# Transposing two steps behind the scores, fetching stored activations by single parts, and stores from a second queue, in a two-layer encoder trunk on one core

## The chip, the core and the metric

The program runs on one of the eight cores of a Trainium2 chip. A core has TensorE (PE in the profile; its weight loads are PEld), VectorE (DVE), ScalarE (ACT), GpSimd (POOL) and SyncE (SP). The metric is the device time of one execution in microseconds (us); lower is better. For one core there are the times of three runs of the kernel before, and one more run under the hardware profiler, from which every row below comes.

## The reference

An encoder trunk of two layers works on two requests of 1024 tokens by 1024 channels that share all weights (`x_prompt` and `x_sample`). All data is 32-bit.

```python
def _trunk(x, c, ...):                       # for each of the two requests
    for i in range(2):
        shift, scale, gate = split(silu(c) @ w_mod[i] + b_mod[i], 3)
        h = _rmsnorm(x, norm_pre[i]) * (1.0 + scale) + shift
        y = _even_mixer(h, ...) if i == 0 else _odd_mixer(h, ...)
        x = x + gate * _rmsnorm(y, norm_post[i])
    return x
def _even_mixer(h, w_in, w_out, ...):        # layer 0
    q, k, v, ga, ub, gb = split(h @ w_in)    # 4 retention heads of 128, 32 S5 groups of 16
    o_a = _head_norm(_retention(_rotary(q), _rotary(k), v)) * silu(ga)
    o_b = _s5(ub, ...) * silu(gb)
    return concatenate([o_a, o_b], -1) @ w_out
def _odd_mixer(h, w_in, w_out, rel_bias):    # layer 1: 16 heads of 64 on a 16 x 64 grid
    q, k, v, g = split(h @ w_in, 4)
    s = q k^T * scale + bias                 # 8 rows x 16 columns of neighbours
    return (softmax(s) @ v * silu(g)) @ w_out
```

## The kernel before

**Products.** Every product with a large weight is made of three: a weight block comes in as `wr`, ScalarE makes `wh` from it (line 198), VectorE or GpSimd the rest `wl = wr - wh` (line 209), and TensorE adds `h_hi wh + h_lo wh + h_hi wl` (`mm`, line 131, 24 instructions for 512 tokens). The normalised input of a layer lies in `h_hi` and `h_lo`, one pair of 1024 tokens for one request at a time.

**Order.** Python generators stand for the secondary work. `spawn(gen, delay)` puts one in a list, and `unit()`, called after each dense product, takes one step of each; a step that yields n rests for n units. So the dense products of a stage are woven with one step each of the mixers. Most of the program is issued in the order in which it is written (`pin`); the rest is placed by a scheduler that moves instructions whose order isn't pinned.

**Stages.** First both requests are normalised, request 1 in `first` and request 0 in `make_h`; `h_rows` (lines 455 to 460) turns a block of x by TensorE, ScalarE applies scale and shift into a tile `tm`, VectorE and GpSimd make `h_hi` and `h_lo` of it, and for request 1 the tile is also stored to `hD[0]`. Beside them go the modulation products `psa<-wn` and `psc<-wn` of `mod`, whose last part calls `save_gate`, which stores a column of `mods` to `gD`; the projections `ub`, whose results `u` are stored to `uD`; and the parameters of the S5 mixer (`s5_params`), which go through DRAM (`ppD`) and are read back by the generator `s5`, which is woven into layer 0. The queue of SyncE issues all loads and all stores, one after the other, and each waits there until its data or its place is ready (the queue is SPq in the profile, line 191).

When request 0 is through its projections in layer 0, `load_h` brings request 1 back from `hD[0]`: four parts of 256 channels for each half of 512 tokens; each goes to a tile `hraw`, ScalarE copies it to `h_hi` (line 198) and VectorE or GpSimd subtracts to `h_lo` (line 438). Its three places in layer 0 (`hraw`, A12 A13 A14) are those of `kT`, `qT` and `ga` of the retention. Layer 1 does the same from `hD[1]` with `down=True`, there between requests 1 and 0 with a turned grid.

**Layer 1.** `na_dense` makes q, k and the gate of a pair of heads, `na_values` the values of two pairs, and the generator `na_mix` does the attention of one block of 128 queries of a pair of heads in each step: `na_scores` makes the scores in two banks `psa`; VectorE adds the bias and finds the largest (line 1203), ScalarE takes the exponential and its sum (line 1205), VectorE the reciprocal and the product (lines 1206 and 1207); one step later `na_turn` lets TensorE transpose the result into banks `psb` (line 136), and ScalarE and VectorE copy them to tiles `pt` (lines 198 and 1223); then products `psc` with the values are made for two blocks at once. The last steps run beside the output projection of layer 1 (`out_proj`), in which each unit has 12 products of 128 x 512; its own work on VectorE and GpSimd stands in lines 1116 and 1117.

Of the kernel before, what the change touches and what calls it, by code (L numbers as in the profile page):

```python
# [19 lines left out]
P = 128  # L20
# [8 lines left out]
ROWS, WIDE, EDGE = 16, 368, 256  # L29
# [9 lines left out]
def _parts(text):  # L39
# [31 lines left out]
    vn0=_fulls("A15"), kn=_fulls("A16"), vn1=_fulls("A17"), stf=_fulls("A18"), stb=_fulls("A6"),  # L71
    hraw=_fulls("A12 A13 A14"),
    gy=_fulls("E0 E1"), gz=_fulls("A11 A12 A13 A14"), ghl=_fulls("E2 E3"), gw=_fulls("A0 A1 A3 A4"))
# [44 lines left out]
class Trunk:  # L118
# [70 lines left out]

    def load(self, dst, src, pin=False):  # L190
        i = self.nc.sync.dma_start(dst, src)  # L191
        if pin:
            self.tc.keep_in_program_order(i)

    store = load

    def copy_a(self, dst, src, scale=1.0):
# [96 lines left out]
    def mod(self, l, t):  # L294
        pa = [self.pst("a"), self.pst("c")]
        for n in range(4):
            for h in range(2):
                w = self.t([P, 4, 256], "wn")
                c0 = t * 1024 + 256 * n
                self.load(w, self.I["w_mod"][l, 512 * h:512 * h + 512, c0:c0 + 256].rearrange("(k p) c -> p k c", p=P), pin=True)  # L300
                for k in range(4):
                    self.mm(pa[n // 2][32 * k:32 * k + 32, 256 * (n % 2):256 * (n % 2) + 256], self.cs[:, 4 * h + k], w[:, k],
                            start=(h == 0), stop=(h == 1))
                yield
        r = self.t([P, 1024], "modr")
        for n in range(2):
            self.copy_a(r[:, n * 512:(n + 1) * 512], pa[n])
        p2 = self.pst("b")[:, 0:16].rearrange("p (f s) -> p f s", f=8)
        for f in range(8):
            self.mm(p2[:, f], r[:, f * P:(f + 1) * P], self.sel, start=True, stop=True)  # L310
        self.mod_col(p2, l, t, slice(0, 8))
        if t == 2:
            self.save_gate(l)

# [103 lines left out]

    def load_h(self, saved, after, down=False):

        for half in range(2):
            sl = slice(half * 512, half * 512 + 512)
            for c in range(4):
                raw = self.t([P, 2, 512], "hraw")
                ks = slice(2 * c, 2 * c + 2)
                hi, lo = self.h_hi[:, ks, sl], self.h_lo[:, ks, sl]
                src = saved[256 * c:256 * c + 256]
                if down:
                    for k in range(2):
                        self.load(raw[:, k].rearrange("p (r c) -> p r c", r=ROWS),  # L430
                                  src[k * P:(k + 1) * P].rearrange("p (r c) -> p r c", r=ROWS)[:, :, 32 * half:32 * half + 32])
                    raw = raw.rearrange("p k (r c) -> p k c r", r=ROWS)
                    hi, lo = (z.rearrange("p k (c r) -> p k c r", r=ROWS) for z in (hi, lo))
                else:
                    self.load(raw, src[:, sl].rearrange("(k p) t -> p k t", p=P))
                self.copy_a(hi, raw)
                e = self.nc.gpsimd if c % 2 else self.nc.vector
                e.tensor_tensor(lo, raw, hi.bitcast(F32), SUB)
            yield after

# [6 lines left out]
    def h_rows(self, l, s, g, xs, fs, tags, save=None):  # L447
        nc, Vv = self.nc, self.nc.vector
        sl = slice(g * 512, (g + 1) * 512)
        for f in fs:  # L450
            pt = self.pst(tags[f % len(tags)])
            for i, x in enumerate(xs):
                self.tr(pt[:, i * P:(i + 1) * P], x[:, f * P:(f + 1) * P], self.ident)
            tm = self.t([P, 512], "tm")
            nc.scalar.activation(tm, pt, AF.Identity, bias=self.mods[:, l, 0, f, s:s + 1],
                                 scale=self.mods[:, l, 1, f, s:s + 1])
            hh = self.h_hi[:, f, sl]
            Vv.tensor_copy(hh, tm)  # L458
            e = nc.gpsimd if f % 2 else Vv
            e.tensor_tensor(self.h_lo[:, f, sl], tm, hh.bitcast(F32), SUB)  # L460
            if save is not None:
                self.store(save[f * P:(f + 1) * P, sl], tm, pin=True)

# [55 lines left out]
    def s5_params(self):  # L519
# [138 lines left out]
        V.tensor_copy(pkb[:, :, 32:64], o_im.rearrange("p (a g) i -> p a (g i)", g=2))  # L658
        ppv = self.ppD.rearrange("a p x -> p a x")
        for o, z in ((0, pkb), (128, pkw), (182, pkt)):  # L660
            self.store(ppv[:, :, o:o + z.shape[2]], z)

# [131 lines left out]

    def s5(self):

        st = self.s5_begin(0)
        self.s5_tables(st)
# [21 lines left out]
    def ub(self, s):  # L820
        def item(m):
# [7 lines left out]
            def done():  # L829
                self.store(self.uD[s][m * P:(m + 1) * P].rearrange("i t c -> i (t c)"),  # L830
                           u[0].rearrange("p t c -> p (t c)"))

# [230 lines left out]
    def out_proj(self, l, s, blks, xsrc, xdst, save=None):  # L1063
        nc = self.nc
        gp = None
        for i in range(8):
# [27 lines left out]
            if not l:  # L1094
                self.unit()
            gp = gp or self.gate_row(l, s)
            x = self.t([P, 1024], "ox")
# [63 lines left out]
    def na_start(self):  # L1161
# [5 lines left out]
        for a in range(2):  # L1167
            oth = slice(64 - 64 * a, 128 - 64 * a)
            for _ in range(2):
                self.nc.gpsimd.memset(self.t([P, 1024], f"kl{a}")[oth], 0.0)  # L1170
                self.nc.gpsimd.memset(self.t([P, 384], f"s{a}")[:, WIDE:], 0.0)

# [54 lines left out]
    def na_mix(self):  # L1227
# [3 lines left out]
        n = 8 * 16  # L1231
        for i in range(-2, n + 2):
            k, j = divmod(i + 2, 8)
            if k < 16:
# [8 lines left out]
                elif j == 3 and k < 15:  # L1243
                    raw = self.na_raw((k + 1) % 8)
            if i >= 3 and i % 2:
                for b in (i - 3, i - 2):
                    k, j = divmod(b, 8)
# [9 lines left out]
                if j % 4 == 3:  # L1257
# [3 lines left out]
                    self.store(self.oD[1, s][p * P:(p + 1) * P, sl], o)  # L1261
            if 0 <= i - 1 < n:
                pts[i - 1] = self.na_turn(sbs.pop(i - 1), (i - 1) % 8)
            if 0 <= i < n:
# [49 lines left out]
    def layer0(self, xin):  # L1314
# [22 lines left out]
        self.project(ub[1][2:], "2")  # L1337
        self.s5_params()
        ph, self.ph = self.ph, Phase(MAP_L0, **banks)
        self.xs = [self.t([P, 4, P], f"xs{i}") for i in range(2)]  # L1340
        self.bm = self.t([P, 2, 2, 48], "bm")
        for x in self.xs + [self.bm]:
            nc.gpsimd.memset(x, 0.0)
        self.spawn(self.s5(), 4)
        self.ph, ph = ph, self.ph
# [7 lines left out]
        for s in range(2):  # L1353
# [10 lines left out]
            if s == 0:  # L1364
                self.spawn(self.load_h(self.hD[0], 3), 4)
                self.project(gb[0], "13")
# [23 lines left out]
    def layer1(self):  # L1390
# [19 lines left out]
        for s in range(2):  # L1410
            for p in range(8):
# [3 lines left out]
                if s == 0 and p == 7:  # L1415
                    self.spawn(self.load_h(self.hD[1], 3, True), 2)
                if s == 1 and p == 7:
# [89 lines left out]
```

## Time and profile before

| | us |
|---|---|
| runs | 2287.92, 2291.08, 2293.56 |
| median | 2291.08 |
| profiled execution | 2285.23 |
| its span, first to last instruction | 2283.5 |
| TensorE busy in it | 2183.2 (96%) |
| VectorE busy | 1371.3 (60%) |
| ScalarE busy | 850.4 (37%) |
| GpSimd busy | 786.0 (34%) |

The profiled execution is one of its own beside the three runs. Busy time counts the instructions of an engine, so what is missing from the span of TensorE is time in which it had none to do; whether it worked at its full clock is told by PEclk, the granted share of 2.4 GHz.

### The profile page before, as it was taken

How to read it: one execution, taken by the hardware profiler on the slowest of the kernel's cores; microseconds unless marked ns; L12 is line 12 of the kernel's file. 1: busy time of each engine (PE TensorE's matmuls, PEld its weight loads, DVE VectorE, ACT ScalarE, POOL GpSimd, SP SyncE). 2: the span in 40 equal slices, each digit the busy share in tenths (PEclk: the TensorE clock that was granted, in tenths of full speed). 3: DMA queues.
4: the chain of work that ended last, by engine and by line, in shares of the span. 5: the costliest groups of instructions: out<-in, count | busy, mean ns of one | idle time of the engine just before them, and what ended most of it. 6: DMA issues, size and time to landing. Idle time of an engine off the chain costs nothing.

```text
span 2283.5 us, 35173 instructions
## 1 busy us (share of the span) xinstructions
PE 2183.2 (96%) x13248; PEld 1838.0 (80%) x13248; DVE 1371.3 (60%) x3013; ACT 850.4 (37%) x1842; POOL 786.0 (34%) x670
## 2 busy tenths in 40 slices
PE   6989998998999999999999999998999999998997
PEld 4757877876878988888889898987888888986886
DVE  4826888987899666575344545456545555457322
ACT  4532221323322234343343434455444444444211
POOL 2335555666666221366611111113111102113233
PEclk9999999999999999999999999999999999999999
DMA  9774223224122245535511111224111111114354
GB/s 321 238 231 149 79 70 62 62 76 155 41 70 61 88 147 173 174 130 178 161 55 48 51 54 54 57 60 86 47 54 54 54 54 54 42 57 150 94 138 123
DMA packets 296482, 231.14 MB, mean 101 GB/s; under 512 B 58489, under 2 KB 267769, under 8 KB 296313
## 3 DMA queue, kind: packets, MB, share of 16 engines
q1 hardware_dynamic: 296312, 228.90, 33.7%
q8 instruction: 105, 1.72, 0.3%
q14 instruction: 65, 0.52, 0.1%
HBM read 169.92 MB, written 56.84 MB: 99 GB/s over the span
## 4 chain that ended last, share of the span: by engine, by line
PE 73%; DVE 11%; DMA 8%; POOL 2%; issue 2%; SPq 2%; ACT 2%; DVEq 0%; POOLq 0%; ACTq 0%
PE psd L131 53%; DMA out_y<-h_lo 5%; PE psc L131 4%; PE psa L131 4%; PE psb L136 4%; PE psz L131 2%; SPq L191 2%; DVE E L771 2%; PE psy L131 2%; PE psb L131 2%; DMA oD<-A 1%; POOL E L768 1%; PE pse L131 1%; DVE A L666 1%; ACT h_hi L198 1%
## 5 line engine op out<-in xcount | busy, mean ns | idle before, releaser
L131 PE MATMUL psd<-h_hi,wh 128*128 128x512 f32 x1392 | 555.5, 400 | 0.8 <-DVE h_hi L458 0.5
L131 PE MATMUL psd<-h_lo,wh 128*128 128x512 f32 x1392 | 547.3, 394 | 0.4 <-DVE h_lo L460 0.4
L131 PE MATMUL psd<-h_hi,wl 128*128 128x512 f32 x1392 | 546.1, 392 | 0.0
L131 PEld LDWEIGHTS psd<-h_hi,wh 128*128 128x128 f32 x1392 | 263.7, 190 | 56.3 <-issue 3.8
L131 PEld LDWEIGHTS psd<-h_hi,wl 128*128 128x128 f32 x1392 | 263.1, 189 | 56.8 <-issue 1.2
L131 PEld LDWEIGHTS psd<-h_lo,wh 128*128 128x128 f32 x1392 | 263.8, 190 | 54.6 <-issue 2.9
L131 PE MATMUL psd<-wh,h_hi 128*128 128x256 f32 (+1 forms) x960 | 281.0, 305 | 0.0
L131 PE MATMUL psd<-wl,h_hi 128*128 128x256 f32 (+1 forms) x864 | 252.8, 293 | 0.0
L198 ACT ACTIVATE wh<-wr 128x1024 fp32r<-128x1024 f32 x118 | 124.4, 1056 | 308.5 <-PE psd L131 209.8
L209 POOL TENSOR_TENSOR wl<-wr,wh 128x1024 fp32r<-128x1024 f32 x51 | 125.7, 2464 | 279.9 <-ACT wh L198 279.6
L131 PE MATMUL psd<-wh,h_lo 128*128 128x256 f32 x768 | 214.4, 279 | 0.0
L131 PEld LDWEIGHTS psd<-wh,h_hi 128*128 128x128 f32 x960 | 182.9, 191 | 8.1 <-issue 0.2
L1205 ACT ACTIVATE E<-E,nm 128x368 f32<-128x368 f32 (+1 forms) x256 | 146.3, 572 | 78.2 <-DVE nm L1203 77.9
L131 PEld LDWEIGHTS psd<-wl,h_hi 128*128 128x128 f32 x864 | 163.4, 189 | 3.6
L209 DVE TENSOR_TENSOR wl<-wr,wh 128x1024 fp32r<-128x1024 f32 x67 | 90.5, 1351 | 118.2 <-ACT wh L198 117.9
L1185 POOL TENSOR_TENSOR A<-A,A 128x256 f32<-128x256 f32 (+1 forms) x80 | 55.9, 721 | 267.1 <-DVE nm L1203 262.8
L131 PEld LDWEIGHTS psd<-wh,h_lo 128*128 128x128 f32 x768 | 145.0, 189 | 0.3
L1207 DVE TENSOR_SCALAR E<-E,su 128x368 f32<-128x368 f32 (+1 forms) x256 | 127.8, 501 | 8.7
L1203 DVE CUSTOM_DVE_ANT_0 E<-psa,A 128x368 f32<-128x368 f32 (+1 forms) x256 | 121.0, 504 | 4.8 <-PE psa L131 3.7
L136 PE MATMUL psb<-ident,E 128*128 128x128 f32 x704 | 104.8, 283 | 19.8 <-DVE E L1207 16.4
L393 DVE TENSOR_TENSOR rs<-ss 128x1 f32<-128x1 f32 x64 | 39.6, 619 | 121.6 <-ACT h_lo L1103 60.1
L136 PEld LDWEIGHTS psb<-ident,E 128*128 128x128 f32 x704 | 80.4, 143 | 39.3 <-issue 25.0
(340 smaller groups left out, 4156.3 us busy)
## 6 DMA issues: line engine op xcount, KB each, us to landing
wr<-in_w_in_c SPq DMA_DIRECT2D x64, 512.0 KB
wr<-in_w_in_ab SPq DMA_DIRECT2D x48, 512.0 KB
wr<-oD SPq DMA_DIRECT2D x32, 512.0 KB
wn<-in_w_mod SPq DMA_DIRECT2D x24, 512.0 KB
wm<-in_w_mod SPq DMA_DIRECT2D x8, 1024.0 KB
hD<-A SPq DMA_DIRECT2D x32, 256.0 KB
ox<-in_x SPq DMA_DIRECT2D x16, 512.0 KB
x1D<-ox SPq DMA_DIRECT2D x16, 512.0 KB
```

The source lines that it names most:

```text
L131: i = self.nc.tensor.matmul(*a, **k)
L136: i = self.nc.tensor.transpose(*a, **k)
L191: i = self.nc.sync.dma_start(dst, src)
L198: self.nc.scalar.activation(dst, src, AF.Copy, scale=scale)
L209: e.tensor_tensor(lo, raw, hi.bitcast(F32), SUB)
L393: self.nc.vector.tensor_tensor(rs, ss[:, 0:1], ss[:, 1:2], ADD)
L666: eng.tensor_tensor(dst, x.unsqueeze(3).to_broadcast(sh), y.unsqueeze(2).to_broadcast(sh), op)
L771: Vv.tensor_tensor_scan(t1[:, q], r8, t1[:, q], 0.0, MUL, ADD)
L1185: self.nc.gpsimd.tensor_tensor(b, raw[a][:, c0:c0 + n], mask, ADD)
L1203: Vv.tensor_tensor_reduce(sn, sc[a], bt[a], -1.0, 3.0e38, ADD, ALU.min, nm)
L1205: nc.scalar.activation(sn, sn, AF.Exp, bias=nm, scale=-1.0, accum_out=su)
L1207: Vv.tensor_scalar(sn, sn, su, None, MUL)
```

## The change

1. In `na_mix` the transposes are those of the step before the last one, not of the last one; the products with the values are made in even steps for blocks i-4 and i-3, not in odd ones for i-3 and i-2; the loop has one more step. The tiles `s0` and `s1` of the scores have a third place each, in A21, with a memset for each.
2. `load_h` fetches three parts at its first step, rests, and then handles 2, 1, 1, 2 and 2 parts in one unit each; each part handled starts the fetch of another. Its rest is 4 units in layer 0 (the delay of its spawn was 4) and 2 in layer 1 (2 too). In layer 0 its places are A19 A20 A21, which the modulation weights `wn` have used.
3. `put` issues a store from ScalarE's queue; the stores to `hD` in `h_rows` and those to `uD` use it.
4. `save_gate(0)` is called in `out_proj`; the stores of the S5 parameters to `ppD` move from the end of `s5_params` to the start of `s5`.

```diff
     "E3 pt0 1536 pt0 1536 pt1 1536 pt1 1536 o 2048; A19 pt0 1536 pt1 1536; A20 pt0 1536 pt1 1536;
+    A21 s0 1536 s1 1536; ...
-    hraw=_fulls("A12 A13 A14"),
+    hraw=_fulls("A19 A20 A21"),
...
+    def put(self, dst, src, pin=False):
+        self.load(dst, src, pin, self.nc.scalar)
...
         self.mod_col(p2, l, t, slice(0, 8))
-        if t == 2:
-            self.save_gate(l)
...
-    def load_h(self, saved, after, down=False):
-        for half in range(2):
-            sl = slice(half * 512, half * 512 + 512)
-            for c in range(4):
-                raw = self.t([P, 2, 512], "hraw")
...
-                    self.load(raw, src[:, sl].rearrange("(k p) t -> p k t", p=P))
-                self.copy_a(hi, raw)
-                e = self.nc.gpsimd if c % 2 else self.nc.vector
-                e.tensor_tensor(lo, raw, hi.bitcast(F32), SUB)
-            yield after
+    def load_h(self, saved, wait, down=False):
+        parts = [(half, c) for half in range(2) for c in range(4)]
+        raws = []
+        def fetch():
...
+        for _ in range(3):
+            fetch()
+        yield wait
+        for n in (2, 1, 1, 2, 2):
+            for _ in range(n):
+                half, c, raw = raws.pop(0)
...
                 self.copy_a(hi, raw)
                 e = self.nc.gpsimd if c % 2 else self.nc.vector
                 e.tensor_tensor(lo, raw, hi.bitcast(F32), SUB)
+                fetch()
+            yield
...
             if save is not None:
-                self.store(save[f * P:(f + 1) * P, sl], tm, pin=True)
+                self.put(save[f * P:(f + 1) * P, sl], tm, pin=True)
...
-        for i in range(-2, n + 2):
+        for i in range(-2, n + 3):
...
-            if i >= 3 and i % 2:
-                for b in (i - 3, i - 2):
+            if i >= 4 and i % 2 == 0:
+                for b in (i - 4, i - 3):
...
-            if 0 <= i - 1 < n:
-                pts[i - 1] = self.na_turn(sbs.pop(i - 1), (i - 1) % 8)
+            if 0 <= i - 2 < n:
+                pts[i - 2] = self.na_turn(sbs.pop(i - 2), (i - 2) % 8)
             if 0 <= i < n:
                 k, j = divmod(i, 8)
                 sbs[i] = self.na_scores(self.na[k], first if j == 0 else last if j == 7 else mid, j)
...
-                self.spawn(self.load_h(self.hD[0], 3), 4)
+                self.spawn(self.load_h(self.hD[0], 4), 0)
-                    self.spawn(self.load_h(self.hD[1], 3, True), 2)
+                    self.spawn(self.load_h(self.hD[1], 2, True), 0)
```

**TensorE, the first steps of the attention in layer 1.** `psa` are the scores (256 wide in the first block of a pair of heads, 368 in the next), `psb` the transposes, `psd` the dense products; the lines left out are the rest of 24 dense products. Before:

```order
L131 MATMUL psa_10082<-E_1024_9602,q_1048_9871 128x256
L131 MATMUL psd_10099<-h_hi,wh_9900 128x512
...
L136 MATMUL psb_10137<-ident,E_1023_9598 128x128 x2
L136 MATMUL psb_10141<-ident,E_1023_9598 128x128 x2
L131 MATMUL psa_10145<-kh_1054_9934,q_1047_9868 128x368
```

and now:

```order
L131 MATMUL psa_10085<-E_1025_9604,q_1049_9874 128x256
...
L131 MATMUL psa_10140<-kh_1055_9937,q_1048_9871 128x368
L131 MATMUL psa_10140<-E_1022_9596,q_1048_9871 128x368
L131 MATMUL psa_10141<-kh_1056_9941,q_1049_9874 128x368
L131 MATMUL psa_10141<-E_1025_9604,q_1049_9874 128x368
...
L136 MATMUL psb_10191<-ident,E_1023_9599 128x128 x2
L136 MATMUL psb_10195<-ident,E_1023_9599 128x128 x2
L131 MATMUL psa_10199<-kh_1055_9937,q_1048_9871 128x368
```

The transposes of a block stood behind one run of dense products after its scores; they now stand behind the next block's scores and a second such run.

**SyncE's queue, first stage.** `wn` are the modulation weights in the order of their use, `gD` takes the stored gate, `A<-ppD` brings the S5 parameters back. Before:

```order
L191 DMA gD_72<-mods 128x8x1 x2
L191 DMA wn_1122<-in_w_mod 128x4x256
L191 DMA wn_1128<-in_w_mod 128x4x256
L191 DMA wn_1193<-in_w_mod 128x4x256
L191 DMA wn_1199<-in_w_mod 128x4x256
L191 DMA wn_1232<-in_w_mod 128x4x256
L191 DMA wn_1238<-in_w_mod 128x4x256
L191 DMA A_185_1350<-ppD 128x280 x2
L191 DMA cosT_1570<-in_cosT 128x1024
L191 DMA uD_58<-u_146_1070 128x1024
```

and now:

```order
L191 DMA wn_1272<-in_w_mod 128x4x256
L191 DMA wn_1278<-in_w_mod 128x4x256
L191 DMA wn_1188<-in_w_mod 128x4x256
L191 DMA wn_1194<-in_w_mod 128x4x256
L191 DMA wn_1227<-in_w_mod 128x4x256
L191 DMA wn_1233<-in_w_mod 128x4x256
L191 DMA gD_72<-mods 128x8x1 x2
L191 DMA wn_1333<-in_w_mod 128x4x256
L191 DMA A_185_1348<-ppD 128x280 x2
L191 DMA wn_1339<-in_w_mod 128x4x256
```

The stores of the gate are still among the loads, but they stand behind six more loads of `wn`, and no store of `u` stands there any more. The first three loads `hraw<-hD` come 16 rows further on, behind the last of the `wn` loads; before, they stand some 150 rows later.

**GpSimd, the same stage.** `h_lo` with a tile A is a part of the normalised input (line 460 before, 476 now); the instructions on A_185 and A_186 are the first of the S5 generator and need `A<-ppD`. Before:

```order
L460 TENSOR_TENSOR h_lo<-A_49_280,h_hi 128x512
L460 TENSOR_TENSOR h_lo<-A_46_261,h_hi 128x512
L209 TENSOR_TENSOR wl_1271<-wr_1269,wh_1270 128x1024
L666 TENSOR_TENSOR A_185_1350<-A_185_1350 128x288
L666 TENSOR_TENSOR A_186_1352<-A_185_1350 128x288
```

and now:

```order
L476 TENSOR_TENSOR h_lo<-A_49_280,h_hi 128x512
L680 TENSOR_TENSOR A_185_1348<-A_185_1348 128x288
L680 TENSOR_TENSOR A_186_1350<-A_185_1348 128x288
L698 TENSOR_TENSOR A_186_1350<-A_185_1348,A_186_1350 128x288
L476 TENSOR_TENSOR h_lo<-A_46_261,h_hi 128x512
```

The last part of `h_lo` now stands behind three instructions of S5.

## Rows read from the trace of the kernel before

**Rows 1.** The page, busy time of the engines.

```profile
PE 2183.2 (96%) x13248; PEld 1838.0 (80%) x13248; DVE 1371.3 (60%) x3013; ACT 850.4 (37%) x1842; POOL 786.0 (34%) x670
```

**Rows 2.** Waits of TensorE by what ended them: total us, times, longest.

```profile
PE psb L136 <- DVE E L1207: 16.4, 6, 3.8
PE pse L136 <- POOL E L693: 8.3, 3, 4.8
...
PE psb L136 <- DVE su L1206: 3.4, 1, 3.4
```

**Rows 3.** Stretches: length, busy PE PEld DVE ACT POOL, granted clock, DMA share, GB/s.

```profile
0.00:57.00 57.00, 39.80 (x250) 24.15 (x250) 23.57 (x57) 23.61 (x49) 13.15 (x17) 1.00 0.97 321
114.00:171.00 57.00, 47.86 (x289) 32.64 (x288) 15.69 (x32) 17.55 (x32) 18.63 (x21) 0.94 0.76 230
570.00:627.00 57.00, 53.31 (x347) 45.66 (x347) 48.31 (x81) 16.94 (x41) 36.19 (x36) 0.94 0.16 45
1482.00:1539.00 57.00, 57.00 (x346) 47.81 (x345) 31.75 (x86) 27.33 (x61) 6.70 (x7) 1.00 0.23 61
1539.00:1596.00 57.00, 49.23 (x332) 43.59 (x331) 35.00 (x69) 35.46 (x57) 19.91 (x10) 0.94 0.45 89
2052.00:2109.00 57.00, 48.73 (x314) 39.95 (x312) 38.73 (x93) 26.66 (x62) 19.55 (x12) 0.94 0.47 143
```

**Rows 4.** Timeline of one wait beside the output projection: start, length.

```profile
2106.26 0.39 PE L131 MATMUL psd<-wh,h_hi 128*128 128x512 f32 x1
2108.76 1.41 DVE L1116 SCALAR_TENSOR_TENSOR h_lo<-psd,rs,h_lo 128x512 f32<-128x512 f32 x2
2110.24 2.34 POOL L1117 TENSOR_TENSOR h_lo<-h_lo 128x1024 f32<-128x1024 f32 x1 [2.77 <-DVE su L1206]
2110.27 2.84 DVE L1207 TENSOR_SCALAR E<-E,su 128x368 f32<-128x368 f32 x2
2112.94 1.51 PE L136 MATMUL psb<-ident,E 128*128 128x128 f32 x6 [3.74 <-DVE E L1207]
```

**Rows 5.** Timeline of TensorE, the step before it, without a wait.

```profile
2100.60 2.90 PE L131 MATMUL psd<-ow,h_hi 128*128 128x512 f32 x12
2103.43 1.53 PE L131 MATMUL psc<-A,vn 128*64 128x128 f32 x24
```

**Rows 6.** Stretches behind such waits; columns as in group 3.

```profile
1555.60:1559.10 3.50, 2.98 (x10) 2.82 (x11) 2.98 (x8) 1.46 (x4) 2.63 (x2) 0.51 0.70 109
2112.00:2119.00 7.00, 6.06 (x19) 5.34 (x20) 3.92 (x11) 1.80 (x5) 0.58 (x1) 0.51 0.30 76
```

**Rows 7.** Timeline of ScalarE and TensorE, the load of request 1, layer 0.

```profile
533.89 1.06 ACT L198 ACTIVATE h_hi<-hraw 128x1024 fp32r<-128x1024 f32 x1 [4.50 <-DMA hraw<-hD]
545.08 0.75 PE L136 MATMUL pse<-ident,E 128*128 128x128 f32 x3 [4.81 <-POOL E L693]
```

**Rows 8.** First stage: waits of SyncE's queue up to 250 us.

```profile
SPq L191 <- ACT u L198: 14.1, 4, 7.3
SPq L191 <- DVE mods L371: 13.3, 1, 13.3
```

**Rows 9.** First stage: timeline of TensorE, GpSimd, VectorE and SyncE's queue.

```profile
148.48 1.08 PE L131 MATMUL psa<-wn,cs 128*32 128x256 f32 x8 [6.97 <-DMA wn<-in_w_mod]
140.79 1.27 POOL L460 TENSOR_TENSOR h_lo<-A,h_hi 128x512 fp32r<-128x512 f32 x1 [2.36 <-DVE h_hi L458]
158.35 2.29 POOL L666 TENSOR_TENSOR A<-A 128x288 f32<-128x288 f32 x2
155.93 2.51 DVE L719 COPY A<-A 64x64 f32<-64x64 f32 x2 [15.23 <-DMA A<-ppD]
150.97 0.38 SPq L191 DMA_DIRECT2D cosT<-in_cosT  x1
```

**Rows 10.** First stage: stretches; columns as in group 3.

```profile
128.00:135.00 7.00, 7.00 (x50) 5.63 (x49) 1.80 (x5) 2.88 (x5) 1.69 (x2) 1.00 0.01 3
138.00:147.00 9.00, 3.51 (x19) 2.62 (x17) 1.45 (x3) 1.55 (x2) 1.70 (x2) 0.94 0.59 34
```

More of the change, by code (lines that the diff above doesn't have):

```diff
@@ L188, in unit, with load @@
                 self.step(task)
-    def load(self, dst, src, pin=False):
-        i = self.nc.sync.dma_start(dst, src)
+    def load(self, dst, src, pin=False, queue=None):
+        i = (queue or self.nc.sync).dma_start(dst, src)
         if pin:
@@ L417, in h_tile @@
                 self.store(save[512 * q:512 * q + 512, ts].rearrange("(f p) t -> p f t", p=P), tm)
-    def load_h(self, saved, after, down=False):
-        for half in range(2):
-            sl = slice(half * 512, half * 512 + 512)
-            for c in range(4):
-                raw = self.t([P, 2, 512], "hraw")
-                ks = slice(2 * c, 2 * c + 2)
-                hi, lo = self.h_hi[:, ks, sl], self.h_lo[:, ks, sl]
-                src = saved[256 * c:256 * c + 256]
+    def load_h(self, saved, wait, down=False):
+        parts = [(half, c) for half in range(2) for c in range(4)]
+        raws = []
+        def fetch():
+            if not parts:
+                return
+            half, c = parts.pop(0)
+            raw = self.t([P, 2, 512], "hraw")
+            src = saved[256 * c:256 * c + 256]
+            if down:
+                for k in range(2):
+                    self.load(raw[:, k].rearrange("p (r c) -> p r c", r=ROWS),
+                              src[k * P:(k + 1) * P].rearrange("p (r c) -> p r c", r=ROWS)[:, :, 32 * half:32 * half + 32])
+            else:
+                self.load(raw, src[:, half * 512:half * 512 + 512].rearrange("(k p) t -> p k t", p=P))
+            raws.append((half, c, raw))
+        for _ in range(3):
[4 more added lines that the diff above has]
+                half, c, raw = raws.pop(0)
+                hi, lo = (h[:, 2 * c:2 * c + 2, half * 512:half * 512 + 512] for h in (self.h_hi, self.h_lo))
                 if down:
-                    for k in range(2):
-                        self.load(raw[:, k].rearrange("p (r c) -> p r c", r=ROWS),
-                                  src[k * P:(k + 1) * P].rearrange("p (r c) -> p r c", r=ROWS)[:, :, 32 * half:32 * half + 32])
                     raw = raw.rearrange("p k (r c) -> p k c r", r=ROWS)
                     hi, lo = (z.rearrange("p k (c r) -> p k c r", r=ROWS) for z in (hi, lo))
-                else:
-                    self.load(raw, src[:, sl].rearrange("(k p) t -> p k t", p=P))
                 self.copy_a(hi, raw)
@@ L658, in s5_params @@
         V.tensor_copy(pkb[:, :, 32:64], o_im.rearrange("p (a g) i -> p a (g i)", g=2))
-        ppv = self.ppD.rearrange("a p x -> p a x")
-        for o, z in ((0, pkb), (128, pkw), (182, pkt)):
-            self.store(ppv[:, :, o:o + z.shape[2]], z)
+        return [(0, pkb), (128, pkw), (182, pkt)]
     def outer(self, eng, dst, x, y, op=MUL):
@@ L793, in s5_out, with s5 @@
             self.store(self.yD[s][gi * 16:gi * 16 + 16].rearrange("i t c -> t i c"), g2[:, s])
-    def s5(self):
+    def s5(self, tables):
+        for o, z in tables:
+            self.store(self.ppD.rearrange("a p x -> p a x")[:, :, o:o + z.shape[2]], z)
         st = self.s5_begin(0)
@@ L829, in done @@
             def done():
-                self.store(self.uD[s][m * P:(m + 1) * P].rearrange("i t c -> i (t c)"),
-                           u[0].rearrange("p t c -> p (t c)"))
+                self.put(self.uD[s][m * P:(m + 1) * P].rearrange("i t c -> i (t c)"),
+                         u[0].rearrange("p t c -> p (t c)"))
             return self.I["w_in_ab"], 2048 + m * P, "VP"[m % 2], evac, done
@@ L1095, in out_proj @@
                 self.unit()
-            gp = gp or self.gate_row(l, s)
+            if not gp:
+                if l + s == 0:
+                    self.save_gate(0)
+                gp = self.gate_row(l, s)
             x = self.t([P, 1024], "ox")
@@ L1170, in na_start @@
                 self.nc.gpsimd.memset(self.t([P, 1024], f"kl{a}")[oth], 0.0)
+            for _ in range(3):
                 self.nc.gpsimd.memset(self.t([P, 384], f"s{a}")[:, WIDE:], 0.0)
@@ L1337, in layer0 @@
         self.project(ub[1][2:], "2")
-        self.s5_params()
+        tables = self.s5_params()
         ph, self.ph = self.ph, Phase(MAP_L0, **banks)
@@ L1343, in layer0 @@
             nc.gpsimd.memset(x, 0.0)
-        self.spawn(self.s5(), 4)
+        self.spawn(self.s5(tables), 4)
         self.ph, ph = ph, self.ph
```

2 rows, old and new, of the table MAP_L1 are left out of this document.

## The prediction

> **What bounds the kernel now.** I read the page's busy times first: TensorE has work in 2183.2 of 2283.5 us [rows 1], so at most 100.3 us of its idle time can be won, and whatever the other engines save counts only where it ends a wait of TensorE. Then the waits of TensorE by what ended them, then stretches of 57 us to find where they lie, then the timelines there. In the middle of layer 1 TensorE is busy 57.00 of 57 us [rows 3]: nothing is to be won there, and every us won or lost ahead of it passes to the end. Idle time lies in four places.
>
> - The transposes of the attention: 16.4 us in six waits for VectorE's product (line 1207) and 3.4 us in one for its reciprocal (line 1206), 19.8 us in all [rows 2]. The stretches show where: 7.8 us are missing at 1539 to 1596, where request 0 is loaded, and 8.3 us at 2052 to 2109 [rows 3]; the last 3.74 us come just behind that, in the output projection [rows 4].
> - Lost clock behind these waits: the granted clock is 0.51 (that is 1.2 GHz, not 2.4) for 3.5 us behind a gap and for 7 us behind the last one [rows 6]. There are five such stretches in layer 1, four of 3.5 us (of which one row stands here) and that one.
> - Layer 0's load of request 1: ScalarE waits twice for `hraw`, once 4.50 us, and TensorE then 4.81 us for GpSimd [rows 7]; its waits for that line are 8.3 us in three [rows 2], and the stretch from 570 loses 6% of its clock [rows 3].
> - The first stage: 17.2 of the first 57 us with the DMA engines 97% busy, and 9.1 us between 114 and 171 [rows 3], of which 6.97 us for one modulation weight `wn` [rows 9].
>
> **The change, part by part.**
>
> *Two steps between scores and transposes.* In the timeline of the last wait the scores are done at 2106.26, when the dense products begin, and the transposes start at 2112.94 [rows 4]: 6.7 us. In between TensorE has one run of 12 dense products, 2.83 us (2100.60 to 2103.43, [rows 5]). VectorE lies late: two instructions of the output projection take 1.41 us, and its two products, begun at the same time as GpSimd's addition of 2.34 us, take 2.84 us [rows 4]. With the new order the room is one run, a whole step and no wait: 2.83 us + (2106.26 - 2100.60 = 5.66 us) = 8.5 us. That is 1.8 us more than the 6.7 us needed. Beside `load_h` the runs have 24 products, so the room is larger still. I take all 19.8 us as gone; bounds 0 and 19.8.
>
> TensorE, VectorE and ScalarE compute with the same instructions; the two memsets on GpSimd come long before. The products with the values keep their distance of a step from the copies that they read, so nothing is added there. What is late next in the output projection is the bank `psa`: the next scores need line 1203 to have read the last ones. I take 2 us of new waits, between 0 and 13 (the rival below).
>
> *The clock.* Without the gaps the clock has no reason to fall. 3.5 us at 0.51 lack 1.7 us of full clock, 7 us lack 3.4 [rows 6]: 4 x 1.7 + 3.4 = 10.2 us at most. TensorE was idle for a part of these (2.98 of 3.50, 6.06 of 7.00 us busy), which makes it 4 x 1.5 + 3.0 = 9.0. I take 9; bounds 0 and 10.2.
>
> *Layer 0's load.* With three parts fetched long before, right behind the last modulation weights and into places that the retention doesn't use, ScalarE's waits go. But GpSimd's own order is unchanged around the longest wait, and GpSimd was working without a pause before it, so I leave the 4.81 us in. The other two waits, 8.3 - 4.8 = 3.5 us, and half of the slow clock (0.06 x 57 = 3.4 us), together 5 us, I take as won; bounds 0 and 10. The conversions themselves (1.06 us on ScalarE each) are the same eight.
>
> *First stage.* `wn` loads now stand ahead of the gate's store, so they can come in the stretch at 128 to 135 us, in which the DMA engines moved 3 GB/s because SyncE stood 13.3 us before that store [rows 8, 10]. The 6.97 us at 141 should go, and with them some 3.4 us of lost clock (0.06 x 57 in the stretch from 114, [rows 3]). The stores of `u` no longer hold SyncE for 14.1 us [rows 8]. ScalarE pays: 16 stores to `hD` and 8 to `uD` are 24 issues, by SyncE's 0.38 us for one [rows 9] 9 us spread over 200 us, of which it is busy less than half (23.6 and 17.6 of 57 us, [rows 3]); the data are its own results, so it hardly waits for them. Against that stand two new waits. The slow DMA that follows the gate's store (34 GB/s for 9 us, [rows 10]) now hits `A<-ppD`, and GpSimd has three S5 instructions that need it ahead of the last `h_lo`. And `hraw<-hD` waits in SyncE's queue for three places of `wn`, with S5's copies and weights behind it. I take 5 us won, between 12 won and 12 lost.
>
> `s5_params` and the later call of `save_gate` cost nothing by themselves: the same stores, issued elsewhere, with the consequences just counted.
>
> The Trainium skill, page "DMA: Bandwidth & Descriptors", section "Issuing engines are not separate DMA queues", says that DMAs issued from several engines share the same 16 DMA engines and that issuing them elsewhere saves only the sequencer's time. It speaks against the move of the stores: in the first 57 us the DMA engines are 97% busy [rows 3], and no order of issue adds to that. The waits of SyncE's queue for `u` and `mods` are of another kind, an instruction that stands before others, and there the DMA engines are idle, 1% in 128 to 135 [rows 10]. By the page alone the first stage would gain nothing.
>
> **The sum**, against the profiled execution of 2285.2 us: -19.8 - 9.0 + 2.0 - 5.0 - 5.0 = -36.8, so 2248.4 us. The median of the runs is 5.9 us above the profiled execution (2291.1), so I name 2254 us for a median.
>
> **The rivals.**
>
> 1. *The first stage gains nothing*: the bytes to be moved ahead of 140 us are the same, and they set when `wn` is there, in whatever order they are issued. For it: 97% in the first stretch. Against it: 1% at 128 to 135. 2254 + 5 = 2259 us. Chance 0.15. The Trainium skill's page "DMA: Bandwidth & Descriptors" would lead to this one.
> 2. *Everything is won*: layer 0's load 10, the start 12, no new waits, the clock 10.2, the transposes 19.8: 52 us, 2233 in the profile, 2239 as a median. For it: SyncE's waits are long. Against it: GpSimd's unchanged order. Chance 0.12.
> 3. *Half of the attention's gain comes back as waits for `psa` or for h_lo.* VectorE works 38.7 us of 57 in the stretch from 2052 [rows 3]; without the 8.3 us of waits it would be 38.7 of 48.7, 80%, and two blocks of 1.41 + 2.84 us [rows 4] in neighbouring steps leave it behind. `load_h` in layer 1 also gives its last two parts a unit later. (19.8 + 9 - 2) / 2 = 13.4 back: 2268 us. Chance 0.14.
> 4. *GpSimd stands before the last `h_lo`*, the case on the other side. The S5 instructions need `ppD`; today it is there at 155.93, when VectorE's wait of 15.23 us ends, and today the last `h_lo` starts at 140.79 [rows 9]. If it comes no earlier, `h_lo` is done only after 155.9 + 2.3 for two S5 instructions + 1.2 for a third like them + 1.3 = 160.7 [rows 9], some 19 us later than now, of which TensorE's present wait of 7 us is taken away: the start loses 12 instead of gaining 5, 2271 us. Each us beyond costs one: the whole is slower than before if `ppD` arrives later than about 156 + 20 = 176 us. For it: the order; against it: `ppD`'s stores are early, and 34 GB/s ended by 147. Chance 0.11, of which 0.05 slower than before.
> 5. *The waits only change place*: each us won at the transposes is waited again at the scores, and the rest comes to nothing. 2286 to 2291. For it: VectorE's work is the same; against it: it is idle for 20% even then. Chance 0.08.
>
> **How the numbers follow.** My forecast (2244 to 2266) has 0.40; with the five rivals that is 1. Something under 0.3%, 7 us, can't be told from no change here. Faster: forecast, 1, 2, 3 and 0.06 of 4, 0.87; same: 5, 0.08; slower: 0.05. The range reaches from below the case in which everything is won (2236) to above that of GpSimd's wait (2279); it leaves out rival 5, the slow part of 4 and a little below.
>
> **What the changed profile would show.** Right: no wait of `psb` for lines 1206 and 1207 above 1 us, TensorE 57 of 57 us in the stretch of the second load, granted clock 1.00 from there to the last tiles; ScalarE without a wait for `hraw` at layer 0's load; no wait of 7 us for `wn` before 150. Wrong: a wait of `psa` for line 1203 in the output projection, TensorE waiting for `h_lo` of GpSimd near 150 us, or SyncE held before `hraw<-hD` while S5's copies are due. The prediction fails most easily in the first 200 us, where the scheduler gave a new order and no row shows what it costs.

## The result, and the profile after

The changed kernel takes 2258.56 us (median of four runs, 2256.17 to 2261.23) against 2291.36 us for the kernel before measured beside it: a ratio of 0.9858, 95% interval 0.9841 to 0.9876, 32.8 us less. Forecast were 2254 us and a range of 2236 to 2279. The profiled execution's span is 2257.0 us, against 2283.5.

Its page gives TensorE's busy time in the first row, and its waits by what ended them follow (total us, times, longest):

```profile
PE 2178.5 (97%) x13248; PEld 1833.4 (81%) x13248; DVE 1379.2 (61%) x3013; ACT 846.7 (38%) x1842; POOL 788.7 (35%) x672
```

```profile
PE psb L136 <- DVE A L1012: 9.8, 3, 3.8
PE psz L131 <- DVE E L756: 7.1, 5, 2.7
PE psa L131 <- DMA wm<-in_w_mod: 7.1, 2, 6.3
PE psd L131 <- DVE h_hi L474: 5.8, 2, 5.5
PE psz L131 <- issue: 5.7, 1, 5.7
```

The two waits of [rows 2] for lines 1207 and 1206 (now 1227 and 1226) are gone; two stand near its head, one for `h_hi` and one for `psz` (a bank of S5's products) that the profile gives no releaser (`issue`); the second was there before too, with 3.16 us. The stretches that answer to [rows 3] (length, busy PE, PEld, DVE, ACT, POOL, granted clock, DMA share, GB/s; the last two lie over the output projection, which now comes earlier):

```profile
114.00:171.00 57.00, 51.17 (x306) 35.94 (x305) 19.91 (x36) 18.14 (x32) 23.26 (x28) 0.94 0.73 213
570.00:627.00 57.00, 51.35 (x343) 44.12 (x342) 48.44 (x81) 16.23 (x40) 35.43 (x35) 0.97 0.18 50
1539.00:1596.00 57.00, 56.84 (x432) 51.08 (x431) 38.05 (x82) 39.07 (x65) 22.75 (x12) 1.00 0.50 100
2024.00:2081.00 57.00, 55.59 (x357) 45.50 (x356) 43.45 (x108) 31.10 (x72) 16.98 (x10) 1.00 0.50 153
2081.00:2138.00 57.00, 57.00 (x317) 46.85 (x316) 23.79 (x58) 17.20 (x44) 16.55 (x10) 1.00 0.39 107
```

Beside the load of request 0 TensorE now has work for 56.84 of 57 us where it had 49.23, and the granted clock is 1.00 in all three stretches of layer 1. The stretch from 114 has 3.3 us more work than before (51.17 for 47.86) at the same clock; the one from 570 has less (51.35 for 53.31) at a higher clock (0.97 for 0.94).

How the room of two steps is used shows in a timeline of the output projection (start, length; VectorE's line 1227 has the number 1207 before):

```profile
2085.22 0.39 PE L131 MATMUL psd<-wh,h_hi 128*128 128x512 f32 x1
2088.65 0.41 DVE L1227 TENSOR_SCALAR A<-A,su 128x368 f32<-128x368 f32 x1
2089.51 0.87 PE L136 MATMUL psb<-ident,E 128*128 128x128 f32 x6
2093.65 0.82 PE L136 MATMUL psb<-ident,A 128*128 128x128 f32 x6
```

The block whose scores lie in the new place in A21 (the tile A) has them done at 2085.22, VectorE is through with it at 2089.06, and its transposes start at 2093.65: 8.4 us of room, where the prediction worked out 8.5. The transposes at 2089.51 are those of the block before.

What layer 1 gained can be read between one common instruction, the first scores, and the end of the span. Its row before, after and in lag_only (a run below):

```profile
1172.24 0.28 PE L131 MATMUL psa<-kh,q 128*128 128x256 f32 x1
```

```profile
1174.86 0.28 PE L131 MATMUL psa<-kh,q 128*128 128x256 f32 x1
```

```profile
1175.39 0.28 PE L131 MATMUL psa<-kh,q 128*128 128x256 f32 x1
```

From there to the end it was 2283.5 - 1172.2 = 1111.3 us, and is 2257.0 - 1174.9 = 1082.1: 29.2 us won. In no_lag and lag_only (runs below) this part takes 1110.3 and 1082.7 us. Ahead of it the changed kernel is 2.6 us late, where the prediction had 10 won. That is no loss that could be told from none: lag_only, which has the instructions of the kernel before there, is 3 us late too, and two executions of one kernel (gate_rows and gate_rows_b below) lie 7.8 us apart at this row (1157.10 and 1164.89).

In the first stage the timelines of TensorE, VectorE and GpSimd show what took the place of the wait for `wn` [rows 9]:

```profile
149.78 0.80 PE L131 MATMUL psd<-h_hi,wh 128*128 128x512 f32 x1 [5.49 <-DVE h_hi L474]
```

```profile
148.02 0.83 DVE L733 COPY A<-A 64x64 f32<-64x64 f32 x2 [10.89 <-DMA A<-ppD]
148.89 0.83 DVE L474 CAST h_hi<-A 128x512 fp32r<-128x512 f32 x1
```

```profile
148.13 1.31 POOL L680 TENSOR_TENSOR A<-A 128x288 f32<-128x288 f32 x2 [9.64 <-DMA A<-ppD]
149.52 0.87 POOL L698 TENSOR_TENSOR A<-A,A 128x288 f32<-128x288 f32 x1
151.35 1.28 POOL L476 TENSOR_TENSOR h_lo<-A,h_hi 128x512 fp32r<-128x512 f32 x1 [0.97 <-DVE h_hi L474]
```

VectorE and GpSimd each have an S5 instruction that needs `ppD` ahead of the last `h_hi` and `h_lo`, and stand before it for 10.89 and 9.64 us. TensorE waits 5.49 us for `h_hi`, in place of 6.97 for `wn`. Behind the gate's store the transfers are slow, as before [rows 10]:

```profile
135.00:138.00 3.00, 3.00 (x16) 2.22 (x16) 2.10 (x3) 0.78 (x1) 2.03 (x2) 1.00 0.94 31
138.00:147.00 9.00, 6.29 (x52) 3.21 (x48) 0.00 (x0) 2.04 (x3) 0.49 (x1) 1.00 0.68 80
```

The DMA engines are 94% and 68% busy and move 31 and 80 GB/s.

What the first stage won, and where that went, shows at two like products of S5 in layer 0, on both sides of the second gate's store. Before, and then now:

```profile
372.71 1.08 PE L131 MATMUL psz<-E 128*64 128x256 f32 x8
383.91 1.09 PE L131 MATMUL psz<-E 128*64 128x256 f32 x8 [3.16 <-issue]
```

```profile
368.53 1.08 PE L131 MATMUL psz<-E 128*64 128x256 f32 x8
382.27 1.97 PE L131 MATMUL psz<-E 128*64 128x256 f32 x8 [5.70 <-issue]
```

At the first of them TensorE stands 4.2 us earlier than before, at the second 1.6. The runs lag_only and no_lag, which differ in the same parts there, have 371.49 and 369.69, then 382.44 and 381.70: 1.8 us, then 0.7. So the changed first stage had won 2 to 4 us by then, and most of it was waited again at the second product.

### The profile page after: what moved, and what is told of

It reads as the page before. It is cut to its first block, busy times and chain, and to the rows that moved or that the text cites. A ratio compares the mean times of both kernels' runs of the same rounds, so it can differ in the third digit from the quotient of the medians.

```text
span 2257.0 us, 34972 instructions
## 1 busy us (share of the span) xinstructions
PE 2178.5 (97%) x13248; PEld 1833.4 (81%) x13248; DVE 1379.2 (61%) x3013; ACT 846.7 (38%) x1842; POOL 788.7 (35%) x672
## 3 DMA queue, kind: packets, MB, share of 16 engines
HBM read 169.92 MB, written 56.84 MB: 100 GB/s over the span
## 4 chain that ended last, share of the span: by engine, by line
PE 74%; DVE 10%; DMA 7%; POOL 3%; ACT 2%; issue 2%; SPq 2%; DVEq 0%; ACTq 0%; POOLq 0%
PE psd L131 54%; PE psc L131 4%; PE psa L131 4%; PE psb L136 4%; DMA out_y<-h_lo 3%; PE psz L131 2%; SPq L191 2%; PE psy L131 2%; PE psb L131 2%; DVE E L785 1%; DMA oD<-A 1%; DVE A L680 1%; POOL E L782 1%; DMA h_lo<-x1D 1%; ACT h_hi L202 1%
## 5 line engine op out<-in xcount | busy, mean ns | idle before, releaser
L1225 ACT ACTIVATE E<-E,nm 128x368 f32<-128x368 f32 (+1 forms) x172 | 98.0, 571 | 52.9 <-DVE nm L1223 52.7
L1243 DVE COPY A<-psb 128x384 f32<-128x384 f32 x64 | 33.5, 523 | 122.5 <-PE psb L136 121.2
L785 DVE TENSOR_TENSOR_SCAN E<-A,E 128x128 f32<-128x128 f32 x128 | 88.9, 754 | 31.2 <-POOL E L782 30.8
L680 POOL TENSOR_TENSOR A<-A 128x288 f32<-128x288 f32 (+1 forms) x128 | 91.6, 735 | 32.7 <-DVE E L728 14.6
L1205 POOL TENSOR_TENSOR A<-A 128x368 f32<-128x368 f32 x16 | 13.9, 890 | 254.0 <-DVE nm L1223 253.4
```

What stands on the lines that cost most here:

```text
L680: eng.tensor_tensor(dst, x.unsqueeze(3).to_broadcast(sh), y.unsqueeze(2).to_broadcast(sh), op)
L785: Vv.tensor_tensor_scan(t1[:, q], r8, t1[:, q], 0.0, MUL, ADD)
L1205: self.nc.gpsimd.tensor_tensor(b, raw[a][:, c0:c0 + n], mask, ADD)
L1225: nc.scalar.activation(sn, sn, AF.Exp, bias=nm, scale=-1.0, accum_out=su)
L1243: self.nc.vector.tensor_copy(pt, pp)
```

## The experiments

Four questions: which part of the change wins the 32.8 us; where the 10 us of the first stage and of layer 0 went; whether the gate's store is to blame, and by its place or by its form; and whether the other parts win anything once it is out of the way. The ratios are those to the kernel before, each beside runs of it on the same chip. Its medians beside them were 2288.18 to 2292.06 us, so between runs of different rounds the ratio tells more than a difference of 2 to 4 us in the medians.

| kernel | median us | ratio, 95% interval |
|---|---|---|
| the changed kernel | 2258.56 | 0.9858 (0.9841 to 0.9876) |
| lag_only | 2258.71 | 0.9860 (0.9845 to 0.9874) |
| no_lag | 2288.01 | 0.9997 (0.9985 to 1.0010) |
| gate0_late | 2243.50 | 0.9793 (0.9778 to 0.9807) |
| gates_late | 2247.99 | 0.9812 (0.9795 to 0.9828) |
| lag_gate0 | 2244.95 | 0.9816 (0.9791 to 0.9840) |
| gate_rows | 2243.11 | 0.9804 (0.9785 to 0.9823) |
| lag_rows | 2245.14 | 0.9815 (0.9799 to 0.9831) |
| gate_rows_b | 2243.16 | 0.9791 (0.9770 to 0.9811) |
| rows_no_put | 2246.61 | 0.9806 (0.9790 to 0.9822) |
| rows_old_load | 2243.80 | 0.9791 (0.9775 to 0.9808) |

**lag_only and no_lag: the lag alone, and all but the lag.** The first adds the `na_mix` lines of the change, the places in A21 and the memsets to the kernel before:

```diff
-        for i in range(-2, n + 2):
+        for i in range(-2, n + 3):
-            if i >= 3 and i % 2:
-                for b in (i - 3, i - 2):
+            if i >= 4 and i % 2 == 0:
+                for b in (i - 4, i - 3):
-            if 0 <= i - 1 < n:
-                pts[i - 1] = self.na_turn(sbs.pop(i - 1), (i - 1) % 8)
+            if 0 <= i - 2 < n:
+                pts[i - 2] = self.na_turn(sbs.pop(i - 2), (i - 2) % 8)
```

> The kernel before with part 1 of the change alone (transposes two steps behind, third places for the scores). Theory: the lag alone removes the 19.8 us of waits for the transposes and the 9 us of slow clock behind them, so it is 25 to 29 us faster than before (about 2264), no wait of TensorE for line 1207 is left, and up to layer 1 it runs as before. Rival: the three waits beside the load of request 0 in layer 1 (7.8 us and two slow stretches) went because that load is spread over more units; then they stay here and the gain is 15 to 18 us (about 2275).

The second takes these lines back out of the changed kernel.

> The changed kernel with part 1 undone (transposes one step behind, two places for the scores). Theory: it loses the 25 to 29 us again and stands within 7 us of the kernel before (about 2285 to 2288), with the waits for line 1207 back in the load of request 0 and in the output projection. Rival: the spread load alone keeps the first three waits away, and it loses only 15 to 18 us (about 2275).

The lag alone gives the whole gain: 0.9860 against 0.9858, some 32 us and so a little more than the theory's 25 to 29. Without it there is none, 0.9997. The waits of TensorE in layer 1 (1150 to 2200 us) decide between theory and rival. In no_lag, with the load spread over five units:

```profile
PE psb L136 <- DVE E L1226: 16.1, 7, 3.8
PE psb L136 <- DVE su L1225: 3.4, 1, 3.4
```

and in lag_only, with the old load of four parts at once:

```profile
PE psd L131 <- ACT h_hi L198: 0.6, 1, 0.6
PE psb L136 <- DVE A L1224: 0.4, 1, 0.4
PE psd L131 <- DVE h_lo L1116: 0.3, 1, 0.3
```

Spreading the load leaves 19.5 of the 19.8 us, the lag leaves 1.3 of all waits. The theory stands, and the rival falls.

**gate0_late and gates_late: the stores of the gates out of the way.** VectorE copies the gate's columns late, and the store is made from the copy:

```diff
     def save_gate(self, l):
+        g = self.gcol[l]
+        self.tc.keep_in_program_order(self.nc.vector.tensor_copy(g, self.mods[:, l, 2]))
         for s in range(2):
-            self.store(self.gD[l][s].rearrange("(f p) -> p f", p=P), self.mods[:, l, 2, :, s])
+            self.store(self.gD[l][s].rearrange("(f p) -> p f", p=P), g[:, :, s])
...
         assert len(self.bg) == 1, self.bg
+        self.save_gate(0)
```

The second run also takes the call for layer 1 out of `mod_blocks` and puts it at the start of `layer1`.

> The changed kernel, but the first gate's column is copied by VectorE late in layer 0 and stored from there, so that its store no longer stands among the loads of the first stage; everything else keeps its order there. Theory: TensorE's wait of 5.5 us at 144 us comes from the S5 parameters, which land late behind that store, so this wait and the slow clock after it (6.83 us at half) go and TensorE stands 8 to 10 us earlier at the last modulation product; but most of that is waited again in layer 0, whose S5 chain ends no earlier, and the whole is only 0 to 4 us faster than the changed kernel (2255 to 2259). Rival: what is won in the first stage passes to the end, 2249 to 2251.

> As the run before it, and the second gate's store, which stands at 364 us in layer 0, is moved to the start of layer 1 in the same way. Theory: the wait of 5.7 us at 376 us comes from the slow transfers behind that store, which hold S5's copies; without it this wait falls below 1 us and the slow clock behind it goes, 5 to 9 us more than the run before it (2248 to 2253). Rival: S5's copies are slow by themselves (9.9 us for eight before the change as well), the wait stays, and the time is that of the run before it within 2 us.

In gate0_late the first half of the theory holds, the second doesn't: the wait at 144 us goes, and what is won passes to the end, even more than the rival had, 15.1 us by the medians. VectorE waits for `ppD` for 3.54 us instead of 10.89, and the first stage is nearly full (stretch 114 to 171):

```profile
140.20 0.84 DVE L735 COPY A<-A 64x64 f32<-64x64 f32 x2 [3.54 <-DMA A<-ppD]
```

```profile
114.00:171.00 57.00, 56.65 (x360) 39.68 (x359) 22.34 (x43) 21.06 (x39) 27.45 (x32) 1.00 0.77 260
```

This is the store at work on like transfers: SyncE issues the two loads of `ppD` at the same time in the changed kernel and in gate0_late, and VectorE has them 9.5 us later (148.02) in the one and 2.2 us later (140.20) in the other.

```profile
138.51 0.81 SPq L191 DMA_DIRECT2D A<-ppD  x2
```

```profile
138.03 0.81 SPq L191 DMA_DIRECT2D A<-ppD  x2
```

The other part of the gain came unplanned: the second gate's store, whose call stayed where it was but which is now made from a copy too, falls behind S5's copies `E<-E` and not ahead of them, and the wait of 5.70 us at 382 is gone. The two products shown above start at 360.34 and 368.31: 8.2 us earlier than in the changed kernel, then 14.0. gates_late expected that from moving this store, and was a miss: the wait was gone already. At the store's new place, at the start of layer 1, TensorE waits 2.15 us for VectorE, and the kernel is 4.5 us slower by the medians than gate0_late; the intervals overlap, so the loss isn't shown.

```profile
1146.95 0.47 PE L131 MATMUL psd<-h_hi,wh 128*128 128x512 f32 x1 [2.15 <-DVE q L1170]
```

Its trace points to the store, though no run tried it: the two transfers are issued at 1116.04 and 1117.94, SyncE's next load only at 1127.44 (1115.86 in gate0_late), and the weight block behind it is so late that ScalarE, for which VectorE waits, stands before it for 9.75 us:

```profile
1140.21 1.06 ACT L202 ACTIVATE wh<-wr 128x1024 fp32r<-128x1024 f32 x1 [9.75 <-DMA wr<-in_w_in_c]
```

**lag_gate0: is the late store enough for the lag alone?** The same edit of the first gate, made to lag_only.

> The kernel before with part 1 (the lag) and with the first gate stored late in layer 0 as in gate0_late, but with the old load_h, all stores on SyncE's queue and the S5 parameters stored where they were. Theory: the stores on ScalarE's queue and the parts fetched ahead are worth nothing, only the gate's store hid a gain: it comes within 4 us of gate0_late (2240 to 2248). Rival: with that store out of the way the other parts of the change do win; then this one lacks 5 to 10 us of it (2249 to 2254).

2244.95 us: as the theory has it, within 1.5 us of gate0_late. By the ratios, 0.9816 and 0.9793, it would be 5 us, with intervals that overlap; so a gain of a few us from the other parts isn't excluded here, and none is shown.

**gate_rows and lag_rows: the store in its place, in another form.** TensorE turns the gate's column, ScalarE copies it, and one transfer of 16 pieces of 512 bytes takes the place of 2048 of 4 bytes:

```diff
-    def save_gate(self, l):
+    def save_gate(self, l, tag):
+        pt = self.pst(tag)
         for s in range(2):
-            self.store(self.gD[l][s].rearrange("(f p) -> p f", p=P), self.mods[:, l, 2, :, s])
+            self.tr(pt[0:8, s * P:(s + 1) * P], self.mods[:, l, 2, :, s], self.ident)
+        g = self.grow[l]
+        self.copy_a(g, pt[0:8, 0:2 * P].rearrange("f (s p) -> f s p", s=2))
+        self.store(self.gD[l].rearrange("s (f p) -> f s p", p=P), g)
```

> The changed kernel with both gates stored where the kernel before stores them, at the end of their modulation products, but as rows: TensorE turns the column (two products of 128 x 8), ScalarE copies it, and one transfer of 16 pieces of 512 bytes takes the place of two of 1024 pieces of 4 bytes. Theory: it is the pieces of 4 bytes that slow the transfers behind them; so both waits go (5.5 us at 144 and 5.7 us at 376) with the slow clock behind them, and it is 14 to 20 us faster than the changed kernel (2239 to 2245). Rival: what delays the parameters is that SyncE stands before the store until the gate is ready; then the wait at 144 stays and it is only 0 to 6 us faster (2253 to 2259).

> The kernel before with part 1 (the lag) and both gates stored as rows, nothing else. Theory: the waits in the first stage have two causes here, SyncE standing 13 us before the store and the slow transfers behind it; only the second goes, so it lies between lag_only and gate_rows, 2245 to 2253. Rival: only the slow transfers count, and it equals gate_rows within 3 us.

gate_rows is 15.4 us faster than the changed kernel by the medians and 12 by the ratios, with the store still among the loads. It also moves the last `h_lo` on GpSimd and the last `h_hi` on VectorE back ahead of S5's instructions, and the six loads of `wn` behind the store again, as the scheduler places them, so order and form can't be told apart in this run alone. lag_rows against lag_only tells them apart: both have the order and the place of the kernel before. TensorE's wait for `wn` in lag_only, then in lag_rows:

```profile
PE psa L131 <- DMA wn<-in_w_mod: 7.4, 1, 7.4
```

```profile
PE psa L131 <- DMA wn<-in_w_mod: 0.8, 1, 0.8
```

So in the first stage it is the form of the store and not its place. The stretch behind the store, and the eight copies `E<-E` in SyncE's queue, in gate_rows:

```profile
136.00:145.00 9.00, 9.00 (x66) 4.61 (x65) 2.11 (x5) 2.67 (x4) 2.65 (x4) 1.00 1.07 385
```

```profile
357.78 5.20 SPq L191 DMA_DIRECT2D E<-E  x8
```

and these copies in the kernel before, then in the changed kernel:

```profile
369.56 9.88 SPq L191 DMA_DIRECT2D E<-E  x8
367.06 10.50 SPq L191 DMA_DIRECT2D E<-E  x8
```

385 GB/s where there were 80, and 5.2 us for the copies where there were 10.5. The two stretches don't hold the same transfers (the six loads of `wn` stand ahead of the store in the changed kernel and behind it here), the copies do. Of the 5.3 us that these take longer, SyncE stands 4.3 until the gate's two transfers, issued at 361.13 and 361.55, have landed (its waits from 335 to 400 us in the changed kernel):

```profile
SPq L191 <- DMA gD<-mods: 4.3, 2, 3.4
```

The third copy starts at 371.81 at the end of such a wait, so a store of 4 KB took about 11 us to land.

lag_rows, the kernel before with two parts alone, equals gate_rows within 2.0 us, as its rival said, and lies at the lower end of its theory's range. What SyncE's stand before the store costs shows against lag_only: it is 14.8 us there and 18.1 in lag_rows,

```profile
SPq L191 <- ACT grow L198: 18.1, 1, 18.1
```

and yet the wait for `wn` falls from 7.4 us to 0.8. So the stand by itself costs next to nothing; the slow transfers behind the store do.

**gate_rows_b, rows_no_put, rows_old_load: the other parts, with the store out of the way.** Stores back on SyncE's queue (`put` without `self.nc.scalar`), and the old load of request 1 in layer 0:

```diff
-                self.spawn(self.load_h(self.hD[0], 4), 0)
+                self.spawn(self.load_h_whole(self.hD[0], 3), 4)
...
-    hraw=_fulls("A19 A20 A21"),
+    hraw=_fulls("A12 A13 A14"),
```

> The same kernel as gate_rows, as the base that the next two are to be compared with on one chip. Expected: 2240 to 2246 again.

> gate_rows with the stores to hD and uD back on SyncE's queue. Theory: nothing behind these stores is late once the gate is a row, so it is within 2 us of gate_rows. Rival: SyncE's waits for u (14 us in the kernel before) hold back loads that TensorE needs in the first 200 us, and it is 4 to 8 us slower.

> gate_rows with the old load of request 1 in layer 0: four parts at one unit, twice, into the places of the retention (the load in layer 1 stays by single parts). Theory: TensorE waits there for S5's work on GpSimd and VectorE, not for the parts, so it is within 2 us of gate_rows. Rival, and the term of the prediction: the parts fetched ahead are worth 5 us, and it is 4 to 8 us slower.

The old load costs nothing: 2243.80 against 2243.16. The stores are between theory and rival: 3.5 us slower, but the intervals overlap (0.9770 to 0.9811 and 0.9790 to 0.9822), so a gain of a few us from ScalarE's queue can't be excluded, and none is shown.

## Why the prediction was right, step by step

**The transposes, 19.8 us: right.** All of it is gone, for the reason given: the room worked out as 8.5 us is 8.4 in the trace, and lag_only and no_lag show that it is the lag and nothing else.

**The clock, 9 us, and new waits, 2 us: right.** The granted clock is 1.00 from 1175 to 2200 us. The new waits there (1150 to 2200 us) are 1.5 us, none of them for `psa` and line 1203:

```profile
PE psd L131 <- ACT h_hi L202: 0.6, 1, 0.6
PE psd L131 <- DVE h_lo L1135: 0.4, 1, 0.4
PE psb L136 <- DVE A L1243: 0.3, 1, 0.3
PE psc L131 <- DVE A L1243: 0.2, 1, 0.2
```

The three terms together were 26.8 us and measured 29.2. The room was measured at one block, so its agreement to 0.1 us is partly chance; that it is more than the 6.7 us needed is not.

**The first stage, 5 us won: nearly right there, wrong for the end.** It was split as 7 us of waiting for `wn` and 3.4 us of clock won, less something for two new waits. The wait for `wn` went, as forecast. The wait that the fourth rival feared came, 5.49 us long, and the clock in 114 to 171 stayed at 0.94. Even so TensorE stood 2 to 4 us earlier at 370 us, as the two products above show. The step that failed is "every us won or lost ahead of it passes to the end": layer 0 has waits of its own, and behind the second gate's store S5's copies `E<-E` ended at 377.6 us where they had ended at 379.4, so that TensorE waited 5.70 us in place of 3.16 and kept 0.7 to 1.6. With the first store out of the way and the second behind those copies (gate0_late) the gain does reach the end.

The rival had named `ppD` behind the gate's store and GpSimd's order; it overlooked that VectorE has such an instruction too, the copy `A<-A`, ahead of the last `h_hi`, and that is what TensorE waited for. `ppD` came at 148.0, not at the 155.9 that the rival feared.

**The load in layer 0, 5 us won: wrong.** ScalarE waited for `hraw` three times before (4.50, 5.39 and 1.33 us), not twice, and still does twice, 3.50 us for the fourth part and 2.25 for the last, since only three places hold parts fetched ahead:

```profile
534.47 1.06 ACT L202 ACTIVATE h_hi<-hraw 128x1024 fp32r<-128x1024 f32 x1 [3.50 <-DMA hraw<-hD]
```

TensorE's waits between 520 and 600 us were 8.3 us for GpSimd's line 693 and 1.8 and 0.2 for others; now they are:

```profile
PE pse L136 <- POOL E L707: 5.1, 2, 3.4
PE psz L131 <- DVE E L756: 4.0, 2, 2.7
PE psd L131 <- DVE A L856: 1.4, 1, 1.4
PE psd L131 <- DVE A L923: 1.2, 1, 1.2
```

11.7 us in place of 10.3: less is waited at `pse`, more at the next results of VectorE. rows_old_load says the same from the other side: it has the wait for GpSimd back at 8.4 us and costs nothing.

**The median.** The sum was 2248.4 for a profiled execution, which measured 2258.76. It was 10.4 us too low, since ahead of layer 1 the changed kernel lost 2.6 for 10 won, and in layer 1 it won 2.4 more than forecast. The median was taken 5.9 us above the profile, because the profiled execution of before lay that far below the median of its runs; the changed kernel's lies at its median. So by the medians the change is worth 32.8 us and by the two profiles 26.5, and the forecast of 2254 came within 4.6 us partly because that allowance wasn't needed. That is luck: it hid more than half of the 10.4 us.

**The rivals.** The first (nothing won in the first stage) has the number that came, 2259, but not the mechanism: bytes do not bind between 114 and 171 us, since gate0_late fills that stretch (56.65 of 57 us) and wins 15 us with the same bytes. In the first 57 us they may: the DMA engines stay 96% busy there in the changed kernel, and TensorE has 39.11 us of work where it had 39.80. The Trainium skill, page "DMA: Bandwidth & Descriptors", section "Issuing engines are not separate DMA queues", gives no bandwidth to a second issuing queue. rows_no_put agrees as far as it goes, with no difference outside the intervals. The same page, section "Specifications", asks for pieces of 512 bytes at least for full rate. gate_rows agrees: it makes such pieces of a store of 8 KB and is 2.0% faster than the kernel before, where the lag alone is 1.4%. That most of this lies in the transfers behind the store is what the runs above show.

## What to carry to other kernels

A producer that is late by a few us now and then, through collisions on its engine, is answered by distance: one more step between scores and transposes cost two small tiles and removed all seven waits and the slow clock behind them. A wait that ends is to be followed to the next one on the same chain, on every engine whose queue holds an instruction for it: here the wait of 6.97 us for weights became one of 5.49 for parameters, and most of what was left was waited again 200 us later behind a second store. What an early stage wins is to be read at a like instruction there and at another further on. And a small store in pieces of 4 bytes is to be judged by what stands behind it in the DMA engines, not by its bytes: turned into rows it won 12 to 15 us more, where the whole change had won 33.

## What was not expected of the hardware

Two stores of 4 KB, in 2048 pieces of 4 bytes, slow what stands behind them, and the second gate's took about 11 us to land. In the first stage two loads of `ppD` issued at 138 us are there 9.5 us later, and 2.2 us later without the store. While they run the DMA engines move 31 and 80 GB/s in the changed kernel's stretches from 135 to 147 us, at a share of busy time of 0.94 and 0.68; 385 GB/s at a share of 1.07 were moved at that place in gate_rows. SyncE needs 10.50 us in place of 5.20 for eight small copies behind such a store. The share of busy time alone, 0.94 at 31 GB/s, would have passed for a full DMA.
